# A streaming-encoder layer: the order of four engines in its first part set by tables

## The chip, the cores and the metric

The kernel runs on one core of a Trainium2 chip. The number that counts is the device time of one execution in microseconds; three executions of the kernel before took 1384.44, 1378.92 and 1384.58 us, median 1384.44. The core has these engines: TensorE (PE: matmuls and transposes; its weight loads are shown apart as PEld), VectorE (DVE), ScalarE (ACT), GpSimd (POOL) and SyncE (SP), which issues most DMAs. Each runs its own list of instructions strictly in the list's order and waits at an instruction until what it needs is there.

## The reference

One layer of an encoder, for 1024 new positions (the prompt) and 64 positions of a running stream with 512 cached ones (the sample). `z = x @ w_in` is split into columns for three groups of heads:

- fox: 6 heads of attention with a forget gate: `softmax(q k / 8 + c_t - c_s)` over the causal keys, then times v
- sgu: `gelu(u) * (tril(w_s) @ layer_norm(gelu(v)) + b_s)` in blocks of 128 positions
- sb ("stick-breaking"): 6 heads with `sigmoid(z_ts) * prod_{s<j<t} (1 - sigmoid(z_tj))`, strictly causal, then times v

The three are put side by side, normalised per head, multiplied by `w_out` and added to x with a layer norm; then come `square(relu(x @ w_up)) @ w_down` and a second layer norm. New keys, values and gates are outputs too. All of it is in float32.

## The kernel before

**Numbers in two pieces.** A float32 operand is split into a high piece (a rounded copy, fp32r) and a low one (the rest), and a product is three matmuls: high by high, high by low, low by high. So a block of weights needs a DMA into a raw buffer, a copy on ScalarE (the high piece) and a subtraction on VectorE or GpSimd (the low piece); `load_w` does it, with two raw buffers of the tag `raw` in turn:

```
nc.sync.dma_start(raw, w_in[:, 4 * g:4 * g + 4, col:col + n])
nc.scalar.activation(hi, raw, AF.Copy)
lo_sub(nc.vector if g in dve else nc.gpsimd, lo, raw, hi)
```

**The first part** (about 0 to 590 us) makes projections and attention. It is written as two generators, woven together by counted costs: F makes the projections of a pair of heads (`kv_stage`, `q_stage`), later `sgu_v` and `sgu_u`; A makes the attention of a pair for 256 queries at a time (`Unit`), and for the sample (`Sample`). Pairs are called fox0 to fox2 and sb0 to sb2 in the names. In a unit of sb, TensorE makes scores (`Ssb`, L567); VectorE adds the mask to the last 128 columns (L574); ScalarE makes sigmoids of plus and minus the scores (`sgsb` L549, `snsb` L550), the mask coming before them; VectorE runs a product scan over `snsb` (L551), GpSimd multiplies (L553); TensorE transposes (`ptsb`, L615); ScalarE copies the high piece (`pthsb`, L583), VectorE subtracts (`pthsb`, L98); TensorE multiplies with the values (`osb`: L625 and L626 use the high piece, L627 and L628 the low one); ScalarE copies out (`osbsb`, L638), TensorE transposes again (`otpsb`, L646). `softmax_rows` (L539, L542) stands in for the scan in fox. For the gating, `sgu_v` makes `g1v` and `sgvv` by steps on ScalarE, VectorE and GpSimd and splits them as `vh` and `vl`. L98 is the helper `lo_sub`, so all subtractions of low pieces have that line.

**The second part** (from 590 us) is the output projection and the two large matmuls of the MLP. Its order is not touched.

**What sets the order.** The program is traced in the woven order and handed to the tile scheduler (`TileContext(schedule_with_timeline_sim=True)`), which works out each engine's list by a simulated timeline, and puts in the semaphores. Only a few pieces are chained by hand (`in_order`), by a dependency that fixes the order on one engine and sets no semaphore.

## Time and profile before

| | |
|---|---|
| three executions | 1384.44, 1378.92, 1384.58 us |
| profiled execution | 1384.7 us, of which its span 1383.0 us |
| mean granted clock of TensorE | 0.988 |
| busy: TensorE, its weight loads | 1318.9 us (95%), 1200.2 us (87%) |
| busy: VectorE, ScalarE, GpSimd | 994.2 us (72%), 719.0 us (52%), 613.7 us (44%) |

How to read rows of the trace: a row of the timeline has start, duration, engine, line, operation, `out<-in`, and count; in brackets stands how long the engine was idle just before it, and what ended that. Buffer numbers are left out, so that `Ssb` is the scores of any sb unit. A row of the waits has engine and line, the thing waited for, total us, times and longest. A row of windows has the stretch, its length, the busy time (and count) of PE, PEld, DVE, ACT and POOL, the mean granted clock of TensorE (1.00 is full), DMA share and GB/s. Where an idle engine is not the bottleneck, its idle time costs nothing by itself.

### The profile page before, as it was taken

To read this page: it belongs to the slowest core of one execution; us is meant where nothing else is said; L and a number is where in the kernel's file an instruction comes from. 1 tells how busy PE (TensorE), PEld (TensorE's weight loads), DVE (VectorE), ACT (ScalarE), POOL (GpSimd) and SP (SyncE) were. 2 spreads that over 40 slices of the span, in tenths; PEclk is the share of its full clock that TensorE was granted. 3 is DMA by queue.
4 is the path that set the end of the run, shared out by engine and by line. 5 is a ranking of instruction groups with operands and counts; after the bars stand their busy time and mean duration, and the time that the engine had idled before them with its cause. 6 is when DMAs were issued, how large, how long until landed. Compare 5 with 4: busy or idle time off the path is not lost.

```text
span 1383.0 us, 24317 instructions
## 1 busy us (share of the span) xinstructions
PE 1318.9 (95%) x8827; PEld 1200.2 (87%) x8827; DVE 994.2 (72%) x1797; ACT 719.0 (52%) x1561; POOL 613.7 (44%) x666
## 2 busy tenths in 40 slices
PE   7999989999898998999999999999998999999996
PEld 7899989999888988778899999999976787887774
DVE  4667566576788279778885877767677777777677
ACT  4457566566556376334523322222267676766665
POOL 3221222255665446766412321221176665655557
PEclk9999999999999999999999999999999999999998
DMA  7445564231303247532244434344568344435233
GB/s 226 107 125 143 165 201 122 59 90 43 103 13 73 64 146 246 171 125 70 77 132 138 159 120 169 127 135 156 178 215 282 122 144 142 141 119 170 87 136 130
DMA packets 158048, 185.64 MB, mean 134 GB/s; under 512 B 27740, under 2 KB 116124, under 8 KB 157928
## 3 DMA queue, kind: packets, MB, share of 16 engines
q1 hardware_dynamic: 155832, 183.01, 41.7%
q8 instruction: 70, 1.15, 0.4%
q10 hardware_dynamic: 2096, 1.07, 0.3%
q14 instruction: 50, 0.41, 0.1%
HBM read 117.65 MB, written 60.10 MB: 129 GB/s over the span
## 4 chain that ended last, share of the span: by engine, by line
PE 56%; DVE 12%; DMA 11%; ACT 8%; POOL 7%; issue 5%; SPq 0%; ACTq 0%; DVEq 0%; POOLq 0%
PE zA L1310 9%; PE zD L1310 6%; PE A L1775 5%; PE kvsb L368 5%; PE mx L251 4%; PE kvfox L368 3%; PE zB L1310 3%; PE zC L1310 3%; DMA rwo<-w_out 3%; POOL wd L98 3%; DMA rd<-w_down 2%; PE D L1775 2%; POOL rd L1442 1%; DMA awa<-h_dr 1%; PE qsb L509 1%
## 5 line engine op out<-in xcount | busy, mean ns | idle before, releaser
L98 POOL TENSOR_TENSOR wa<-wr,wa 128x512 fp32r<-128x512 f32 x41 | 65.2, 1618 | 219.3 <-ACT wa L1248 219.3
L98 POOL TENSOR_TENSOR wd<-rd,wd 128x512 fp32r<-128x512 f32 x77 | 100.5, 1316 | 110.9 <-ACT wd L1248 106.3
L251 PE MATMUL mx<-xT,oTb 128*128 128x512 f32 (+1 forms) x416 | 104.1, 402 | 1.6 <-DVE oTb L98 1.6
L1310 PE MATMUL zD<-xo,ws 128*128 128x288 f32 (+1 forms) x720 | 97.5, 289 | 2.7 <-DVE h4a L1474 1.6
L1310 PE MATMUL zA<-xo,ws 128*128 128x288 f32 (+1 forms) x720 | 97.0, 289 | 0.0
L1310 PEld LDWEIGHTS zD<-xo,ws 128*128 128x128 f32 x720 | 93.5, 189 | 3.4 <-DVE h4a L1474 1.8
L1310 PEld LDWEIGHTS zA<-xo,ws 128*128 128x128 f32 x720 | 93.4, 189 | 0.0
L251 PEld LDWEIGHTS mx<-xT,oTb 128*128 128x128 f32 (+1 forms) x416 | 75.5, 187 | 20.3 <-DVE oTb L98 2.4
L1442 POOL TENSOR_TENSOR rd<-rd 128x512 f32<-128x512 f32 x56 | 79.4, 1418 | 30.2 <-DVE b L98 27.9
L368 PE MATMUL kvfox<-wkvfox,xT 128*128 128x256 f32 (+3 forms) x624 | 89.5, 291 | 2.9 <-ACT wkvfox L344 2.5
L553 POOL TENSOR_TENSOR sgsb<-sgsb,snsb 128x127 f32<-128x127 f32 (+7 forms) x48 | 58.4, 1217 | 75.6 <-DVE snsb L551 68.4
L368 PE MATMUL kvsb<-wkvsb,xT 128*128 128x256 f32 (+1 forms) x624 | 88.5, 287 | 0.0
L1248 ACT ACTIVATE wd<-rd 128x512 fp32r<-128x512 f32 x105 | 63.5, 623 | 46.7 <-POOL rd L1442 23.3
L1775 PE MATMUL A<-wd,wd 128*128 128x512 f32 x312 | 83.3, 396 | 3.2 <-DVE acc L1742 2.3
L368 PEld LDWEIGHTS kvfox<-wkvfox,xT 128*128 128x128 f32 (+1 forms) x624 | 80.8, 191 | 4.2 <-ACT wkvfox L344 2.9
L551 DVE TENSOR_TENSOR_SCAN snsb<-snsb,one 128x128 f32<-128x128 f32 (+7 forms) x48 | 72.3, 1510 | 15.3 <-ACT snsb L550 14.7
L368 PEld LDWEIGHTS kvsb<-wkvsb,xT 128*128 128x128 f32 (+1 forms) x624 | 79.4, 187 | 0.2
L1321 ACT ACTIVATE sn<-zA 128x256 f32<-128x256 f32 (+1 forms) x80 | 30.9, 389 | 89.5 <-PE zA L1310 83.0
L1775 PEld LDWEIGHTS A<-wd,wd 128*128 128x128 f32 x312 | 58.1, 188 | 19.3 <-DVE acc L1742 3.6
L1775 PE MATMUL A<-wd,h4a 128*128 128x512 f32 x240 | 64.7, 395 | 2.2 <-DVE awa L1742 1.3
L1531 ACT ACTIVATE ws<-wr 128x1024 fp32r<-128x1024 f32 x28 | 29.1, 1056 | 56.7 <-DVE wr L1260 56.7
L1775 PEld LDWEIGHTS A<-wd,h4a 128*128 128x128 f32 x240 | 44.6, 188 | 14.3 <-DVE awa L1742 1.7
(551 smaller groups left out, 3744.1 us busy)
## 6 DMA issues: line engine op xcount, KB each, us to landing
h_dr<-hh SPq DMA_DIRECT2D x30, 512.0 KB, 3.2
rd<-w_down SPq DMA_DIRECT2D x30, 512.0 KB, 4.6
wr<-w_up SPq DMA_DIRECT2D x13, 1024.0 KB, 5.5
hr<-h_dr SPq DMA_DIRECT2D x31, 384.0 KB, 4.6
h_dr<-hh SPq DMA_DIRECT2D x30, 384.0 KB, 3.6
raw<-w_in SPq DMA_DIRECT2D x44, 256.0 KB, 3.4
wo_dr<-swo SPq DMA_DIRECT2D x32, 256.0 KB, 2.4
xT<-wo_dr SPq DMA_DIRECT2D x8, 1024.0 KB, 8.0
```

What stands on the lines that cost most here:

```text
L98: eng.tensor_tensor(out, src, hi.bitcast(F32), op=ALU.subtract)
L251: nc.tensor.matmul(acc[0:m], oT[:, k, hx, 0:m], wo[k // 4][hw][:, k % 4, cs], start=(i == 0), stop=(i == len(seq) - 1))
L368: nc.tensor.matmul(acc[0:n, c0:c0 + n1 - n0], xT[k // 4][:, k % 4, c:c + n], wt[:, k, hw, n0:n1], start=(i == 0), stop=(i == len(seq) - 1))
L509: nc.tensor.matmul(acc[:, 0:w], wq[:, k, hw, :], xT[k // 4][:, k % 4, c:c + w], start=(i == 0), stop=(i == len(seq) - 1))
L551: nc.vector.tensor_tensor_scan(g[:, 0:n][:, ::-1], g[:, 0:n][:, ::-1], one.broadcast_to([P, n]), 1.0, op0=ALU.mult, op1=ALU.bypass)
L553: nc.gpsimd.tensor_tensor(s[:, 0:n - 1], s[:, 0:n - 1], g[:, 1:n], op=ALU.mult)
L1248: nc.scalar.activation(hi, raw, AF.Copy)
L1310: nc.tensor.matmul(z, w[:, hw, k], xop(s, bo, hx)[:, k, :], start=(new and k == 0 and j == 0), stop=(k == 3 and j == 2), skip_group_check= ...
L1321: nc.scalar.activation(c, z, AF.Copy)
L1442: eng.tensor_tensor(r[:, o], r[:, x], r[:, y], op=ALU.subtract)
L1531: nc.scalar.activation(ws[:, 0, q, c], src[:, q], AF.Copy)
L1775: nc.tensor.matmul(z, h[:, hx, q, o], wset[self.c % 2][q][:, hw, wb], start=((n in (0, 3) or n == 1 and self.c == 0) and q == 0 and j == 0 ...
```

## The change

After the first part has been traced, a loop goes through the instructions of TensorE, ScalarE, VectorE and GpSimd in it. It sorts them into lanes by the name of the tile that each writes, and takes them from the lanes in the order of a table, `ORDER`: `23e 24e'` means 23 instructions of lane e, then 24 of lane e' (the odd ones). Each is chained to the one before it by the same kind of dependency as in `in_order`. The arithmetic, the tiles and the buffers stay. SyncE's list and the second part are left to the scheduler. Two lines of the tables are shown, of some 80.

```
+ORDER = {}
+TICK = {"PE": {"kv": 0, "pt": 2, "sgm": 2, "mx": 1}, "ACT": {}, "DVE": {"T": 0, "sgvv": 0, "y": 0}, "POOL": {}}
+KIND = {
+    "PE": "a:S b:Ss0 c:Ss1 d:ftp e:kv f:mx g:o h:op i:os j:otp k:pk l:pkc m:pt n:ptn o:pts p:q q:sgm "
+           "r:sgu s:sgv t:wstp u:xtp",
...
+ORDER["PE"] = """
+8u e 8u 23e 24e' 8u k 8u k 14e 4u 2e' 10e 22e' 4u 8e k 4e 7u k 5u 12e 4u 14e' 2u 10e' 8e k 15e k e 14u 24e'
...
+ORDER["ACT"] = """
+2q 2y D 2y D 2y 2D h 2z h 4D g D g 2h 2D g 2D g h D h g h 2D g 2D h 2b h y g 3y b g b n b 2n f b n f 2h g 2a
...
+        traced = nc.cur_bb.bb.instructions
+        phase_1 = len(traced)
...
+        def lane_of(i, eng, code):
+            nm = i.outs[0].bass_ap.tensor.name
+            m = re.match(r"([a-zA-Z]+\\d?)_?(?:fox|sb)\\d(.*)", nm) or re.match(r"([a-zA-Z]+)(.*)", nm)
+            nums, at = re.findall(r"\\d+", m[2]), TICK[eng].get(m[1])
+            return code[m[1]] + ("'" if at is not None and at < len(nums) and int(nums[at]) % 2 else "")
+
+        for eng, e in (("PE", nc.tensor), ("ACT", nc.scalar), ("DVE", nc.vector), ("POOL", nc.gpsimd)):
+            code = dict(w.split(":")[::-1] for w in KIND[eng].split())
+            lanes = {}
+            for i in traced[phase_1:]:
+                if i.engine == e.engine:
+                    lanes.setdefault(lane_of(i, eng, code), []).append(i)
+            prev = None
+            for word in ORDER[eng].split():
+                n, k = re.match(r"(\\d*)(.*)", word).groups()
+                for _ in range(int(n or 1)):
+                    i = lanes[k].pop(0)
+                    if prev is not None:
+                        tc.add_manual_dep(i, prev.name, mybir.DependencyInfo(
+                            mybir.DependencyClass.NoSync, mybir.DependencyReason.DATA), reason="order")
+                    prev = i
+            assert not any(lanes.values()), eng
```

What the tables alter is seen when the engines' lists of both programs are laid side by side. TensorE's list is the same to the last instruction. ScalarE's differs in ten places and VectorE's in ten. GpSimd's differs mostly in that casts and subtractions of the cached values alternate, where four casts came first; SyncE's, which the scheduler still makes, has some DMAs a few places earlier or later. The ScalarE places, in order of time: at the start two small gate-weight copies go behind three large ones and two copies of x; near 113 us a weight copy goes behind an exponential; near 191 us `swo` (a copy of the output weights) goes behind `kc_fox` on ScalarE, and its VectorE step behind a `kc_fox` there; near 277, 356, 441, 446 and 484 us weight copies go two to four places later; near 439 us a `vh` comes ahead of a `g1v`; near 379 us `osbsb` comes ahead of `qssb`, near 496 us `snsb` ahead of a `qdsb`, near 530 us a `g1u` ahead of two others. On VectorE the mask of a score block comes ahead of scans or subtractions near 297, 428, 484, 494 and 523 us; near 383 to 411 us some steps of `sgvv`, `g1v` and a scan swap places; near 568 us two steps of the head norm do. In the lists below a statement's line number is 84 higher in the changed file than before.

ScalarE near 356 us, where the second half of the SGU weights `wv` is copied; `pthsb0` is the high piece of transposed attention rows, `kvssb1` and `kpsb1` are keys and values of the next pair. Before:

```order
L344 ACTIVATE wv_5078<-raw1542_1_5091 128x4x128
L583 ACTIVATE pthsb0_3_1_2_4993<-ptsb0_3_1_2_4988 128x512
L469 ACTIVATE kvssb1_8_5071<-kvsb1_8_5047 64x256
L454 ACTIVATE kpsb1_3_4668<-pksb1_6_5056 64x256
L583 ACTIVATE pthsb0_3_1_3_5004<-ptsb0_3_1_3_5000 128x384
```

And in the changed program:

```order
L667 ACTIVATE pthsb0_3_1_2_4993<-ptsb0_3_1_2_4988 128x512
L553 ACTIVATE kvssb1_8_5071<-kvsb1_8_5047 64x256
L538 ACTIVATE kpsb1_3_4668<-pksb1_6_5056 64x256
L667 ACTIVATE pthsb0_3_1_3_5004<-ptsb0_3_1_3_5000 128x384
L428 ACTIVATE wv_5078<-raw1542_1_5091 128x4x128
```

The copy of `wv` stood ahead of four others and stands behind them.

VectorE near 428 us; `Ssb1_7_1_512` is the mask's addition to the last scores of pair sb1, `snsb1_7_1` the scan of the same rows. Before:

```order
L842 TENSOR_SCALAR sgvv6_6016<-sgvv6_6016,sgst6_6022 128x256
L647 TENSOR_REDUCE otsb1_2_0_5843<-otpsb1_2_1_5984 128x2x64
L375 TENSOR_TENSOR gsv8_6147<-gsv8_6147,sgv8_6118 64x256
L843 TENSOR_TENSOR sgvv6_6016<-sgvv6_6016,gvb_5423 128x256
L98 TENSOR_TENSOR pthsb1_3_0_0_5981<-ptsb1_3_0_0_5976,pthsb1_3_0_0_5981 128x512
L98 TENSOR_TENSOR pthsb1_3_0_1_6037<-ptsb1_3_0_1_6032,pthsb1_3_0_1_6037 128x512
L574 TENSOR_TENSOR Ssb1_7_1_512_6066<-Ssb1_7_1_512_6066,m_sb_107 128x128
L551 SCALAR_TENSOR_TENSOR snsb1_7_1_6073<-snsb1_7_1_6073,one_70 128x1024
```

And in the changed program:

```order
L926 TENSOR_SCALAR sgvv6_6016<-sgvv6_6016,sgst6_6022 128x256
L658 TENSOR_TENSOR Ssb1_7_1_512_6066<-Ssb1_7_1_512_6066,m_sb_107 128x128
L731 TENSOR_REDUCE otsb1_2_0_5843<-otpsb1_2_1_5984 128x2x64
L459 TENSOR_TENSOR gsv8_6147<-gsv8_6147,sgv8_6118 64x256
L927 TENSOR_TENSOR sgvv6_6016<-sgvv6_6016,gvb_5423 128x256
L182 TENSOR_TENSOR pthsb1_3_0_0_5981<-ptsb1_3_0_0_5976,pthsb1_3_0_0_5981 128x512
L182 TENSOR_TENSOR pthsb1_3_0_1_6037<-ptsb1_3_0_1_6032,pthsb1_3_0_1_6037 128x512
L635 SCALAR_TENSOR_TENSOR snsb1_7_1_6073<-snsb1_7_1_6073,one_70 128x1024
```

The mask is five places earlier, and the five stand behind it; the scan keeps its place.

ScalarE right behind that, near 441 to 448 us; `wkvsb2` are the key and value weights of the last pair, whose raw pieces are `raw2694_0` and `raw2694_1`; `vh8_6116`, the high piece of the sample's SGU value, came next after the last row shown. Before:

```order
L344 ACTIVATE wkvsb2_6172<-raw2694_0_6181 128x4x128
L517 ACTIVATE qdsb2_1_6333<-qsb2_1_6270 64x256
L583 ACTIVATE pthsb1_3_1_0_6250<-ptsb1_3_1_0_6245 128x512
L638 ACTIVATE osbsb1_3_0_6170<-osb1_3_0_5975 128x256
L583 ACTIVATE pthsb1_3_1_1_6263<-ptsb1_3_1_1_6258 128x512
L818 ACTIVATE so7_0_6303<-sgm7_0_6299,bs_5421 128x256
L517 ACTIVATE qdsb2_1_6333<-qsb2_1_6270 64x256
L583 ACTIVATE pthsb1_3_1_2_6292<-ptsb1_3_1_2_6287 128x512
L818 ACTIVATE so7_1_6309<-sgm7_0_6299,bs_5421 128x256
L344 ACTIVATE wkvsb2_6172<-raw2694_1_6185 128x4x128
L583 ACTIVATE pthsb1_3_1_3_6344<-ptsb1_3_1_3_6340 128x384
L818 ACTIVATE so7_2_6316<-sgm7_2_6312,bs_5421 128x256
```

And in the changed program, up to `vh8_6116` and what follows it:

```order
L667 ACTIVATE pthsb1_3_1_0_6250<-ptsb1_3_1_0_6245 128x512
L722 ACTIVATE osbsb1_3_0_6170<-osb1_3_0_5975 128x256
L428 ACTIVATE wkvsb2_6172<-raw2694_0_6181 128x4x128
L667 ACTIVATE pthsb1_3_1_1_6263<-ptsb1_3_1_1_6258 128x512
L902 ACTIVATE so7_0_6303<-sgm7_0_6299,bs_5421 128x256
L601 ACTIVATE qdsb2_1_6333<-qsb2_1_6270 64x256
L667 ACTIVATE pthsb1_3_1_2_6292<-ptsb1_3_1_2_6287 128x512
L902 ACTIVATE so7_1_6309<-sgm7_0_6299,bs_5421 128x256
L667 ACTIVATE pthsb1_3_1_3_6344<-ptsb1_3_1_3_6340 128x384
L902 ACTIVATE so7_2_6316<-sgm7_2_6312,bs_5421 128x256
L931 ACTIVATE vh8_6116<-sgvv8_6146 64x256
L428 ACTIVATE wkvsb2_6172<-raw2694_1_6185 128x4x128
```

The copy of the first piece stands three places later, behind `osbsb1_3_0`; that of the second goes behind `pthsb1_3_1_3`, `so7_2` and `vh8`.

More of the change, by code (lines that the diff above doesn't have):

```diff
@@ new lines @@
+t B A g A A' t z a z 2A' r 2t i B t i a g B i A g z a i z A' z B z A a r h A 2t B w A' t A' F g t w A z w z
+t r t A w A t F t B u v 2k a B 4k 2a l k 2B a k a w B r B w a t 2s a B j a B t j w B w r a 2t x B r a t B t
+r a B t a t r B t E a B E t g a t r E B g t i E a i g E B E g i t a t i E B r t g t E B E C g C t E C r E t
+C t q C g q 2C p C p q t g q g u v J n 5C r 2C p J q C p 2s n 2q n q J' J 2p n J J' 2n 2J'
+"""
+ORDER["POOL"] = """
+e 4o 2n p n a n a 12n o m o m 4n p 2a 2n 4d 7n 4k n 4k 2n 4o 2m 2p n 4d 8n 4k 2n 4k 5n 4o 2m 2p 2n 4d 7n 4k
```

69 lines of the change are left out of this document (added).

## The prediction

> **What bounds the kernel now.** I read the page first, then the waits of TensorE, then the busy time on both sides of 590 us, where the tables end.
>
> ```profile
> span 1383.0 us, 24317 instructions
> PE 1318.9 (95%) x8827; PEld 1200.2 (87%) x8827; DVE 994.2 (72%) x1797; ACT 719.0 (52%) x1561; POOL 613.7 (44%) x666
> ...
> 0.00:590.00 590.00, 549.77 (x4246) 522.99 (x4247) 402.79 (x859) 335.04 (x831) 249.70 (x364) 0.98 0.43 124
> 590.00:1383.00 793.00, 769.15 (x4583) 677.21 (x4581) 591.37 (x939) 383.92 (x730) 364.04 (x303) 0.99 0.42 142
> ```
>
> TensorE is busy for 95% of the span, and its order and matmuls do not change. Before 590 us it stands idle for 590.00 - 549.77 = 40.2 us; that is all that an order can win there, besides stretches where TensorE runs at a lower clock. These are its waits before 590 us:
>
> ```profile
> PE osb L627 <- DVE pthsb L98: 5.4, 9, 1.7
> PE Sfox L567 <- DVE mfox L539: 5.2, 5, 2.9
> ...
> PE xtp L324 <- DMA xr<-x_prompt: 4.4, 1, 4.4
> PE kvfox L368 <- ACT wkvfox L344: 2.5, 1, 2.5
> PE sgv L368 <- DVE sgvv L767: 1.9, 1, 1.9
> ```
>
> No row is large. The waits for mfox, sgvv and the first input (11.5 us) have no moved instruction next to them. So the change is a dozen places of 0.1 to 2 us, and each has to be followed to the next wait.
>
> **Weight copies on ScalarE.** An in-order ScalarE stands before a copy whose DMA is still under way, and what TensorE wants stands behind it. The clearest case is the SGU weights:
>
> ```profile
> 356.21 0.63 ACT L344 ACTIVATE wv<-raw 128x512 fp32r<-128x512 f32 x1 [1.72 <-DMA raw<-w_in]
> 357.38 0.39 PE L625 MATMUL osb<-pthsb,vpsb 128*128 128x256 f32 x1 [0.99 <-ACT pthsb L583]
> ```
>
> ScalarE idles 1.72 us, and TensorE 0.99 us for the pthsb behind. With the copy four places later pthsb starts at its inputs: **-1.0 us** (bounds -1.0 and 0; the sgv matmuls, which use wv, waited for sgvv alone in the list above, so the copy has room). Three smaller cases are alike:
>
> ```profile
> 113.49 0.63 ACT L344 ACTIVATE wkvfox<-raw 128x512 fp32r<-128x512 f32 x1 [0.72 <-DMA raw<-w_in]
> 115.31 0.87 PE L615 MATMUL ptfox<-ident,Tfox 128*128 128x128 f32 x6 [0.17 <-ACT Tfox L542]
> 117.25 0.39 PE L625 MATMUL ofox<-pthfox,vpfox 128*128 128x256 f32 x1 [0.60 <-ACT pthfox L583]
> 190.95 0.72 ACT L997 ACTIVATE swo<-rwo,gmx 128x512 fp32r<-128x512 f32 x1 [1.37 <-DMA rwo<-w_out]
> 192.48 0.39 PE L625 MATMUL ofox<-pthfox,vpfox 128*128 128x256 f32 x1 [0.31 <-ACT pthfox L583]
> 193.69 0.39 PE L627 MATMUL ofox<-pthfox,vpfox 128*128 128x256 f32 x1 [0.22 <-DVE pthfox L98]
> ```
>
> Behind 113.49 the two waits hold 0.77 us. Tfox (L542) goes ahead of the copy and gains about half of its 0.72 + 0.63 us: **-0.4**, half of the 0.77. Behind 190.95 only kc_fox is taken out, pthfox still stands behind swo, so of 0.31 + 0.22 = 0.53 us I take **-0.4**. The fourth, at 277 us, I estimate at **-0.1** from the smallest of these waits. Bounds of the three together: -1.4 and 0.
>
> At the start two gate columns go behind the copies of the large weights. The first matmul waited 2.5 us for the last copy (the row above), and now for a gate copy: **+0.1**, up to +0.7 if a large copy finds its DMA late.
>
> **Masks and scans on VectorE.** The largest place, at 428 to 447 us:
>
> ```profile
> 427.96 0.42 DVE L647 TENSOR_REDUCE otsb<-otpsb 128x128 f32<-128x256 f32 x1
> 431.20 0.29 DVE L574 TENSOR_TENSOR Ssb<-Ssb,m_sb 128x128 f32<-128x128 f32 x1
> 432.71 2.29 DVE L551 TENSOR_TENSOR_SCAN snsb<-snsb,one 128x1024 f32<-128x1024 f32 x1 [1.22 <-ACT snsb L550]
> 439.81 0.47 PE L627 MATMUL osb<-pthsb,vpsb 128*128 128x128 f32 x1 [1.67 <-DVE pthsb L98]
> 441.29 0.63 ACT L344 ACTIVATE wkvsb<-raw 128x512 fp32r<-128x512 f32 x1 [1.25 <-DMA raw<-w_in]
> 443.13 0.69 PE L646 MATMUL otpsb<-ident,osbsb 128*128 128x128 f32 x2 [1.04 <-ACT osbsb L638]
> 446.18 0.72 POOL L844 TENSOR_TENSOR sgvv<-sgvv,gvb 64x256 f32<-64x256 f32 x1 [2.09 <-DVE sgvv L843]
> 446.85 0.62 ACT L344 ACTIVATE wkvsb<-raw 128x512 fp32r<-128x512 f32 x1
> 447.43 1.70 PE L368 MATMUL kvsb<-wkvsb,xT 128*128 128x256 f32 x13
> 448.09 0.41 ACT L847 ACTIVATE vh<-sgvv 64x256 fp32r<-64x256 f32 x1
> ```
>
> The mask goes from 431.20 to 427.96, five places up. Its sigmoids are then done before VectorE comes to the scan, and most of the scan's idle 1.22 us goes: VectorE runs about 1.1 us earlier up to the pthsb on which TensorE waits 1.67 us at 439.81. Behind that, the weight copy at 441.29 (1.25 us idle) goes behind osbsb, and most of the 1.04 us at 443.13 goes too. Together -2.1. What is late next: the second weight half (446.85) now stands behind vh of tile 8 (448.09), and vh behind the GpSimd step that ends at 446.18 + 0.72 = 446.90. The kv matmuls start at 447.43; twelve of the thirteen use the first half, the last, at 447.43 + 1.70 less one matmul or about 448.8, the second. If vh's chain comes 1.1 us earlier too, vh runs at about 445.9 and the copy ends at 445.9 + 0.41 + 0.62 = 446.9, so TensorE can gain up to 448.8 - 446.9 = 1.9 us before it waits there. The DMA of that half is issued when the first half's copy and subtraction have freed the slot; that copy's place moves down while the chain moves up, so it stays about where it was. On SyncE its issue then stands behind one more output (o_dr), whose ScalarE step is earlier as well. I take **-1.6**, bounds -2.5 (all the waits and some of the low clock below) and 0 (vh unmoved: the copy then ends at 448.09 + 0.41 + 0.62 = 449.1, 0.3 after the place where it is wanted).
>
> The other masks and scans:
>
> ```profile
> 299.72 1.64 DVE L551 TENSOR_TENSOR_SCAN snsb<-snsb,one 128x512 f32<-128x512 f32 x1 [0.83 <-ACT snsb L550]
> 302.41 0.39 PE L625 MATMUL osb<-pthsb,vpsb 128*128 128x256 f32 x1 [1.56 <-ACT osbsb L638]
> 480.88 3.01 DVE L551 TENSOR_TENSOR_SCAN snsb<-snsb,one 128x256 f32<-128x256 f32 x2
> 483.70 0.63 ACT L344 ACTIVATE wu<-raw 128x512 fp32r<-128x512 f32 x1 [2.31 <-DMA raw<-w_in]
> 488.63 1.70 PE L368 MATMUL sgu<-wu,xT 128*128 128x256 f32 x12 [1.15 <-DVE qdsb L518]
> 494.19 0.33 PE L627 MATMUL osb<-pthsb,vpsb 128*128 128x128 f32 x1 [0.38 <-DVE pthsb L98]
> 494.44 0.60 ACT L549 ACTIVATE sgsb<-Ssb 128x512 f32<-128x512 f32 x1 [1.43 <-DVE Ssb L574]
> 497.09 1.04 PE L567 MATMUL Ssb<-kpsb,qdsb 128*128 128x256 f32 x4 [1.07 <-ACT snsb L550]
> ```
>
> At 299.72 the mask now goes ahead of the scan before; VectorE's 0.83 us idle shrinks, but the mask must wait for its scores: **-0.3** of the 1.56 us (bounds -0.8, +0.3). At 483.70 the copy lets ScalarE go on, but VectorE is full from the two scans at 480.88 onward, and the 1.15 us wait hangs on VectorE: **-0.2** (bounds -1.15, 0). At 494.44 the mask goes ahead of a scan and pthsb: ScalarE's 1.43 us wait and the 1.07 us at 497.09 behind it go, the 0.38 us at 494.19 grows: **-0.6** (bounds -1.1, +0.3). At 523 us the same swap, estimated by half of that: **-0.3**.
>
> ```profile
> 379.11 0.42 PE L646 MATMUL otpsb<-ident,osbsb 128*128 128x128 f32 x2 [1.71 <-ACT osbsb L638]
> 379.74 0.19 PEld L627 LDWEIGHTS osb<-pthsb,vpsb 128*128 128x128 f32 x1 [0.18 <-DVE pthsb L98]
> ```
>
> Here osbsb goes ahead of qssb, and the 1.71 us wait gets shorter, but L627, four matmuls on, waits for VectorE until 379.74 whatever ScalarE does: **0**. The moved products in the SGU values (383 to 411 us) and the last regions (530, 568 us) stand where VectorE is full; together I estimate **-0.3**, bounds +-1.
>
> GpSimd's and SyncE's places also shift (casts and subtractions of cached values now alternate); none of the waits above ends on them, so 0, and 0.5 us if one cover goes.
>
> **Sum**: -1.0 - 0.4 - 0.4 - 0.1 + 0.1 - 1.6 - 0.3 - 0.2 - 0.6 - 0.3 + 0 - 0.3 = -5.1 us. The profiled execution took 1384.7 us (span 1383.0 and 1.7 around it), 0.3 above the median of 1384.44. Forecast: 1384.7 - 5.1 = **1379.6 us**. The bounds of the terms, all the good or all the bad ones, are -10 and +3; they will not fall together, so its own range is 1376.5 to 1382.
>
> **The clock, and the rivals.** The granted clock of TensorE halves in places:
>
> ```profile
> 185.10:188.50 3.40, 0.57 (x4) 0.57 (x5) 2.67 (x8) 2.64 (x7) 0.00 (x0) 1.00 0.48 167
> 439.30:446.10 6.80, 5.26 (x23) 4.96 (x24) 5.07 (x12) 4.23 (x10) 2.73 (x4) 0.50 0.53 122
> 497.20:500.70 3.50, 3.50 (x17) 3.50 (x18) 3.34 (x7) 2.70 (x9) 0.83 (x2) 0.52 0.17 37
> ```
>
> *More gain by the clock.* The stretches at 0.50 and 0.52 follow the very waits that shrink here (437 and 497 us). At full clock their TensorE work would take half: 5.26/2 = 2.6 and 3.50/2 = 1.75 us, 4.4 together, so 1379.6 - 4.4 = 1375.2 us. Against it: the weight copy at 447 holds the first back, and 185.10 shows 3.40 us with only 0.57 busy and the clock at 1.00, so idle alone does not decide. [...]
>
> *Stalls only move.* As at 379.74: VectorE, not the moved instruction, is behind most waits. If only 1.0 at 356 and half a microsecond elsewhere is kept, 1384.7 - 1.5 = 1383.2 us. For it: 488.63; against: the idle 1.22 us of VectorE itself.
>
> *Slower by the second weight half at 446.85.* Standing behind vh, it comes late if GpSimd or a scan of 2.29 us gets between. Once the copy starts after 448.8 - 0.6 = 448.2 us it holds the kv matmuls one for one. Three scans of 2.29 us ahead of vh's VectorE steps would make it 6.9 + 0.3 = 7.2 us late; the other places give -5.1 + 1.6 = -3.5, so 1384.7 + 3.7 = 1388.4 us. For it: GpSimd had been idle for 2.09 us at 446.18, so the chain already lags. Against it: the order puts no scan among those steps.
>
> *The tables change nothing beyond the listed moves,* or less than that: then 1384 us; the built order shows the moves, so little speaks for it.
>
> **How the numbers follow.** Forecast 0.45, more by the clock 0.22, stalls move 0.23, slower 0.07, no effect 0.03. About 0.5% (6.9 us) can be told from no change, so faster means below 1377.5: nearly all of the clock's case and a fifth of the forecast's, 0.30. Slower means above 1391.4: a third of the slower case, and 0.03 because the three times before already span 5.7 us: 0.05. Same: 0.65. The range, 1373.5 to 1385, holds the forecast, the clock's case but its end, and the case of moved stalls.
>
> **What would show it.** Right: TensorE's waits near 357 and 443 us gone, the scan of 432.71 with no idle before it, the matmul of 379.74 at the same distance to its neighbours, 488.63 little changed, idle before 590 us down from 40 to about 35 us. The clock's case: 1.00 where 439.30 and 497.20 had half. Wrong: the kv matmuls near 447 us waiting for wkvsb, or a new wait at the start above 3 us.

## The result, and the profile after

The changed kernel took 1374.78 us (median of 11 runs, 1369.80 to 1381.56); the kernel before, run beside it, 1382.22 us (11 runs, 1378.44 to 1384.95). The ratio is 0.9950 with a 95% interval of 0.9931 to 0.9969: 6.9 us faster, between 4.3 and 9.5. The ratio is not the quotient of the two medians, which would be 0.9946 (7.4 us). One execution of the kernel before, among those beside the last experiment, took 6199.27 us and is left out of all figures. The forecast was 1379.6 us, 5.1 us less than the profiled execution of before; the profiled execution of the changed kernel took 1378.24 us, 6.5 less than before's. The interval reaches to both sides of the 0.5% that can be told from no change.

The page of the changed kernel, and its busy time on both sides of 590 us:

```profile
span 1376.2 us, 24318 instructions
PE 1317.1 (96%) x8827; PEld 1200.1 (87%) x8827; DVE 996.0 (72%) x1797; ACT 719.7 (52%) x1561; POOL 617.1 (45%) x666
...
0.00:590.00 590.00, 553.52 (x4271) 527.65 (x4272) 407.83 (x865) 337.14 (x833) 258.63 (x368) 0.98 0.43 124
590.00:1376.00 786.00, 763.53 (x4558) 672.45 (x4556) 588.18 (x932) 382.52 (x729) 358.46 (x298) 1.00 0.42 143
```

TensorE's idle time in the first 590 us is 590.00 - 553.52 = 36.5 us, where it was 40.2. The mean clock there is 0.98 in both kernels; behind 590 us it is 1.00 instead of 0.99. Its waits before 590 us, the longest ones:

```profile
PE osb L711 <- DVE pthsb L182: 6.6, 7, 1.7
...
PE Sfox L651 <- DVE mfox L623: 3.8, 3, 2.5
PE kvfox L452 <- ACT wkvfox L428: 3.0, 1, 3.0
PE otpsb L730 <- ACT osbsb L722: 1.8, 2, 1.0
PE otpsb L730 <- DVE otsb L731: 1.7, 1, 1.7
```

In each row stand the sum, the number and the longest of the waits. The wait for `pthsb` of VectorE, the largest before (5.4 us in 9 waits), has grown to 6.6 in 7. What shrank is spread over many small rows.

TensorE's list is the same in both programs, so each matmul can be looked up in both traces and the difference of its start read as a running account. These starts are from the timelines of TensorE; a negative shift means that the changed kernel is ahead.

| matmul | before, us | after, us | shift |
|---|---|---|---|
| first `kvfox` | 8.89 | 9.33 | +0.44 |
| `otpfox` | 105.86 | 107.78 | +1.92 |
| scores behind the `mfox` wait | 187.93 | 189.25 | +1.32 |
| near 235 us | 235.00 | 235.07 | +0.07 |
| `osb` behind the scan at 300 us | 302.41 | 302.00 | -0.41 |
| `osb` behind the `wv` copy | 357.38 | 355.73 | -1.65 |
| `otpsb`, ScalarE's swap | 379.11 | 377.26 | -1.85 |
| near 413 us | 413.31 | 412.10 | -1.21 |
| `osb` with the 1.67 us wait | 439.81 | 438.23 | -1.58 |
| `otpsb` behind the weight copy | 443.13 | 440.04 | -3.09 |
| last `kvsb` matmul, second weight half | 448.85 | 445.84 | -3.01 |
| first `sgu` | 488.63 | 485.45 | -3.18 |
| `osb`, high piece | 494.19 | 491.06 | -3.13 |
| twelve `sgu` | 497.93 | 493.07 | -4.86 |
| `osb` behind them | 500.75 | 494.73 | -6.02 |
| `osb` | 534.86 | 528.12 | -6.74 |
| `mx`, the tables' end | 590.81 | 585.42 | -5.39 |
| end of span | 1383.0 | 1376.2 | -6.8 |

The rows of the changed kernel's timeline that answer to those of the prediction:

```profile
107.78 0.44 PE L730 MATMUL otpfox<-ident,osbfox 128*128 128x128 f32 x2 [1.62 <-ACT osbfox L722]
302.00 0.38 PE L709 MATMUL osb<-pthsb,vpsb 128*128 128x256 f32 x1 [0.77 <-ACT osbsb L722]
355.73 0.36 PE L709 MATMUL osb<-pthsb,vpsb 128*128 128x256 f32 x1
377.26 0.41 PE L730 MATMUL otpsb<-ident,osbsb 128*128 128x128 f32 x2 [1.72 <-DVE otsb L731]
406.93 0.39 PE L709 MATMUL osb<-pthsb,vpsb 128*128 128x256 f32 x1 [1.05 <-ACT pthsb L667]
438.23 0.33 PE L711 MATMUL osb<-pthsb,vpsb 128*128 128x128 f32 x1 [1.67 <-DVE pthsb L182]
440.04 0.63 PE L730 MATMUL otpsb<-ident,osbsb 128*128 128x128 f32 x2
445.84 0.39 PE L452 MATMUL kvsb<-wkvsb,xT 128*128 128x256 f32 x1 [0.37 <-ACT wkvsb L428]
485.45 1.70 PE L452 MATMUL sgu<-wu,xT 128*128 128x256 f32 x12 [0.65 <-DVE qdsb L602]
491.06 0.33 PE L711 MATMUL osb<-pthsb,vpsb 128*128 128x128 f32 x1 [0.54 <-DVE pthsb L182]
493.07 1.69 PE L452 MATMUL sgu<-wu,xT 128*128 128x256 f32 x12
```

Gone are the waits at 357 us (0.99), 443 us (1.04) and 497 us (1.07), smaller the ones at 302 (1.56 to 0.77) and 488 us (1.15 to 0.65). The 1.67 us at 439 is the same to the hundredth, the 1.71 at 379 now has another releaser, and at 445.84 and 406.93 there are new ones. The first 235 us gave nothing: the account starts with a loss of 1.9 us and is back at zero there. Behind the tables' end the account gains another 1.4 us (-5.4 at `mx`, -6.8 at the end of the span), 1.2 of it idle time of TensorE in a part whose order was not touched; in the kernels below that part alone differs from before's by +1.0 to -3.7 us. So a difference of a few us between two executions is no proof of an order; what the moves themselves do is compared step by step over all kernels in the section on the prediction.

### The profile page after: what moved, and what is told of

It reads as the page before. It is cut to its first block, busy times and chain, and to the rows that moved or that the text cites. A ratio compares the mean times of both kernels' runs of the same rounds, so it can differ in the third digit from the quotient of the medians.

```text
span 1376.2 us, 24318 instructions
## 1 busy us (share of the span) xinstructions
PE 1317.1 (96%) x8827; PEld 1200.1 (87%) x8827; DVE 996.0 (72%) x1797; ACT 719.7 (52%) x1561; POOL 617.1 (45%) x666
## 3 DMA queue, kind: packets, MB, share of 16 engines
q8 instruction: 70, 1.15, 0.4%
q10 hardware_dynamic: 2096, 1.07, 0.3%
## 4 chain that ended last, share of the span: by engine, by line
PE 56%; DVE 14%; DMA 10%; ACT 8%; POOL 7%; issue 5%; SPq 0%; ACTq 0%; DVEq 0%; POOLq 0%
PE zA L1419 9%; PE zD L1419 6%; PE mx L335 5%; PE kvsb L452 5%; PE A L1884 5%; PE kvfox L452 3%; PE zB L1419 3%; DMA rwo<-w_out 3%; PE zC L1419 3%; DMA rd<-w_down 2%; PE D L1884 2%; POOL wd L182 2%; PE qsb L593 2%; DVE snsb L635 1%; POOL rd L1551 1%
```

## The experiments

The theories were these. *The listed places*: the gain is the sum of the stalls that the moved masks and weight copies take away, each where the prediction put it. *The clock*: the stalls matter less than the half-speed stretches behind them. *Stalls move*: VectorE and GpSimd set the pace, and what is taken away in one place stands in the next. All kernels compute the whole result. A kernel with before's order written as tables carries single moves; line numbers differ by one to three from kernel to kernel. Ratios are to the kernel before, run on the same chip, with 95% intervals; 0.001 is 1.4 us. Like the ratio above they are not quotients of medians. Where two experiments are compared through their ratios, the intervals are added in quadrature.

### Masks alone

Before's order, with the five masks on VectorE (297, 428, 484, 494, 523 us) and ScalarE's swap of `snsb` and `qdsb` at 496 us. The place at 494 us:

```diff
 DVE scan snsb_3_0
 DVE knsb
+DVE mask Ssb_3_1_0
 DVE scan snsb_2_1
 DVE subtraction pthsb_0_1_0
-DVE mask Ssb_3_1_0
```

> Only the five masks on VectorE (297, 428, 484, 494, 523 us) and the ScalarE swap near 496 us are in their new places; all other lists are as before. By the sum of the prediction: -0.3 - 1.1 (the mask's part of 428 us) - 0.2 - 0.6 - 0.3 = -2.5 us, 1382.2 - 2.5 = 1379.7, and TensorE's step at 439.81 comes 1.1 us earlier against its neighbours ahead of 428 us. By the new reading of the changed trace (GpSimd's power step and the scan get in each other's way there): only -0.4 at 439.81, but -1.5 at 497.09, together about -2.6. If stalls only move: under -0.5. If the clock is behind the gain: -2 to -4, with the stretch at 497 us at full clock.

Measured: 1378.00 us, ratio 0.9983 (0.9970 to 0.9996), 2.3 us faster. Timeline of this kernel:

```profile
298.58 0.39 PE L710 MATMUL osb<-pthsb,vpsb 128*128 128x256 f32 x1 [0.75 <-ACT osbsb L723]
437.36 0.33 PE L712 MATMUL osb<-pthsb,vpsb 128*128 128x128 f32 x1 [1.67 <-DVE pthsb L183]
438.91 0.63 ACT L429 ACTIVATE wkvsb<-raw 128x512 fp32r<-128x512 f32 x1 [1.31 <-DMA raw<-w_in]
440.74 0.69 PE L731 MATMUL otpsb<-ident,osbsb 128*128 128x128 f32 x2 [1.71 <-ACT osbsb L723]
```

The mask at 297 us works: the wait behind it is 0.75 us instead of 1.56. At 428 us the mask alone gains nothing that lasts: 437.36 still waits 1.67 us, and at 440.74 the wait behind the weight copy has become longer, 1.71 us instead of 1.04, because the copy still stands ahead of `osbsb` and its DMA comes no earlier.

### Weight copies alone

Before's order, with the moved weight copies (113, 191, 277, 356, 441, 446 and 484 us). At 441 us:

```diff
-ACT wkvsb, first half
 ACT qdsb
 ACT pthsb_3_1_0
 ACT osbsb_3_0
+ACT wkvsb, first half
```

> Only the weight copies on ScalarE are later (113, 191 with its VectorE step, 277, 356, 441, 446, 484 us); masks and all else as before. By the sum: -0.4 - 0.4 - 0.1 - 1.0 - 0.2, and -0.5 to -1.2 at 443 us, -2.6 to -3.3 us, so about 1379.3; the matmul of 357.38 without a wait, and the first user of the second half of wkvsb2 (448.85) waiting little. If stalls only move: -1 at most, a new wait of the same size within 5 us behind each place. If the second half behind vh is the next bound (the slower rival): a wait over 1 us at 448.85.

Measured: 1378.28 us, ratio 0.9973 (0.9958 to 0.9988), 3.7 us faster. Timeline of this kernel:

```profile
353.57 0.36 PE L710 MATMUL osb<-pthsb,vpsb 128*128 128x256 f32 x1
437.91 0.63 PE L731 MATMUL otpsb<-ident,osbsb 128*128 128x128 f32 x2
443.47 0.39 PE L453 MATMUL kvsb<-wkvsb,xT 128*128 128x256 f32 x1 [0.40 <-ACT wkvsb L429]
```

At 356 us TensorE gains 1.23 us on the matmul before, at 441 us 1.24 us, and both waits are gone, with no mask moved. The second weight half makes TensorE wait 0.40 us at 443.47: here too it is the next bound.

### All other moves alone

Before's order with what is in neither of the two: the gate copies at the start, the swaps at 379, 439 and 530 us, the products of the SGU values at 383 to 411 us, the head norm at 568 us and GpSimd's casts.

> Only the moves to which the prediction gave about nothing: the gate copies at the start, osbsb ahead of qssb (379 us), vh ahead of g1v (439 us), g1u (530 us), the VectorE steps of the SGU values (383 to 411 us) and of the head norm (568 us), and GpSimd's alternating casts. By the sum: +0.1 + 0 - 0.3, so 1382 +- 1. By the changed trace: +0.4 to +1.3 at the start, +0.4 at 383 to 411 us, so 1383 to 1384.

Measured: 1383.51 us, ratio 1.0019 (1.0005 to 1.0033), 2.6 us slower. The timeline shows a first matmul that starts at 9.30 us behind a wait of 2.99 for ScalarE, and two waits near 410 us:

```profile
408.22 0.50 PE L897 MATMUL sgm<-vh,wst 128*128 128x256 f32 x2 [0.41 <-DVE sgvv L850]
411.89 0.44 PE L767 MATMUL pkcsb<-ident,cache_sb_k 128*128 128x128 f32 x2 [1.37 <-DVE otsb L730]
```

The profiled execution of this kernel, 1380.75 us, is the fastest of its twelve, so its trace can hardly show where the loss lies. The three parts add to -2.3 - 3.7 + 2.6 = -3.4 us, against -6.9 of the whole. Their intervals reach 1.8 to 2.1 us to each side, so the sum is known to about 3.4 us and the difference of 3.5 us to about 4.3: whether the parts add up is not decided.

### The change without the place at 428 to 448 us

The changed kernel with before's order there: VectorE's mask, ScalarE's `vh` and `g1v`, both halves of `wkvsb`.

> The changed kernel with the moves of 428 to 448 us alone taken back (the mask, vh4 and g1v8, both halves of wkvsb2). By the sum it loses 1.6 us: 1374.8 + 1.6 = 1376.4, and TensorE loses 1.6 to 1.8 us between 428 and 450 us and keeps the rest. If stalls only move, it loses under 0.5.

Measured: 1377.76 us, ratio 0.9969 (0.9957 to 0.9982). Timeline of this kernel:

```profile
438.99 0.47 PE L710 MATMUL osb<-pthsb,vpsb 128*128 128x128 f32 x1 [1.67 <-DVE pthsb L181]
442.35 0.69 PE L729 MATMUL otpsb<-ident,osbsb 128*128 128x128 f32 x2 [1.08 <-ACT osbsb L721]
```

The wait behind the weight copy is back (1.08 us), the 1.67 us is there as always. By the ratios the place is worth 0.0019, 2.6 us, known to 3.2; by the account of TensorE's starts 3.01 - 1.21 = 1.8 us between 413 and 449 us.

### The change without the start, without the SGU products, without all other moves

The question was what makes the other moves 2.6 us slower. First the changed kernel with before's order at the start alone (ScalarE's copies of the gate columns and of x, the subtractions on GpSimd):

```diff
+ACT wkvfox gate columns, head
 ACT wkvfox raw_0
+ACT xT, first
+ACT wkvfox gate columns, tail
 ACT wkvfox raw_1
```

> The changed kernel with the start alone taken back: the two gate copies on ScalarE and their subtractions on GpSimd stand where they stood before. If the start is what made the leftover moves slower, it gains 0.4 us at the first matmul and up to 1 us more because full clock then comes earlier: 1374.8 - 1 = 1373.8. If the start costs only the +0.1 of the prediction, no difference.

Measured: 1375.18 us, ratio 0.9945 (0.9924 to 0.9966).

Then with before's order of the SGU products on VectorE, 383 to 411 us:

> The changed kernel with the VectorE moves of 383 to 411 us alone taken back (the low half of wst, the products of sgvv, g1v and a scan). If they are what made the leftover moves slower, it gains 1 to 2 us on the changed kernel, 1373 to 1374, and TensorE has no wait of 1.05 us at 406.93. If they cost nothing, as the prediction has it, no difference.

Measured: 1375.35 us, ratio 0.9948 (0.9929 to 0.9967).

Then without all of them:

> The changed kernel with all the moves that the prediction gave about nothing taken back (start, 379, 383 to 411, 530, 568 us, GpSimd's alternating casts), except vh4 ahead of g1v8, which belongs to 428 to 448 us. If the parts add up as they were measured alone (masks -2.4, weight copies -3.7, the leftover moves +2.6 us), it gains 2.6 us on the changed kernel: about 1372. If the parts only work together, it is no faster than the changed kernel, 1374.8, or slower.

Measured: 1375.28 us, ratio 0.9936 (0.9916 to 0.9957). All three are the changed kernel's 0.9950 within their intervals. So the other moves bring nothing in the whole change, and no one of the two larger groups costs what they cost together in before's order. The account of starts gives 0.5 us to the start and 0.4 to the SGU products in the kernel with all other moves alone, 0.9 us together, inside the 0.7 to 4.6 measured; where the rest of the 2.6 us is stays open.

### The output weights behind the attention weights

In the changed kernel and in the one without the other moves the next waits before 200 us stand behind copies of the output weights `swo` on ScalarE:

```profile
190.49 0.74 PE L652 MATMUL Sfox<-kpfox,qdfox 128*128 128x256 f32 x4 [2.70 <-DVE mfox L624]
108.94 0.44 PE L731 MATMUL otpfox<-ident,osbfox 128*128 128x128 f32 x2 [1.69 <-ACT osbfox L723]
```

These rows are from the timeline of the kernel without the other moves; in the changed kernel the waits are 2.5 (the `mfox` row of its waits) and 1.62 us. The wait near 107 us is not the order's alone: the kernels without the place at 428 us and without the start, whose order is the same there, do not lose these 1.3 us. The obvious step is the change's own: move the copy (and VectorE's step for it) behind what TensorE wants.

```diff
-ACT swo_1 (107 us)
 ACT osbfox_2_0
 ACT kvsfox_7
 ACT pthfox_2_1_0
 ACT pthfox_2_1_1
+ACT swo_1
...
-ACT swo_1 (186 us)
 ACT kc_fox_0
 ACT osbfox_2_1
...
 ACT pthfox_3_0_1
+ACT swo_1
```

> The changed kernel, and two copies of output weights (swo1_1 near 107 us, swo5_1 near 186 us in its profile) stand behind the attention work that is ready, on ScalarE and on VectorE. TensorE's waits of 1.62 us (otpfox) and 2.47 us (Sfox behind mfox) should go, 3 to 4 us: 1371 to 1372. If stalls only move, the later output weights hold the next copy, and the gain is under 1 us.

Measured: 1382.01 us, ratio 0.9995 (0.9979 to 1.0011): all of the gain is lost, 6.2 us (known to 3.4) against the changed kernel. Both waits are gone, and this stands in their place in the timeline (the row SPq is the issue of a load on SyncE's queue):

```profile
188.31 0.42 SPq L1073 DMA_DIRECT2D rwo<-w_out  x1
192.24 0.72 ACT L1080 ACTIVATE swo<-rwo,gmx 128x512 fp32r<-128x512 f32 x1 [4.08 <-DMA rwo<-w_out]
193.50 0.58 PE L708 MATMUL ofox<-pthfox,vpfox 128*128 128x256 f32 x1 [3.87 <-ACT pthfox L666]
```

The load of the next raw piece is issued at 188.31, when the one before is done with (VectorE's step for it ends at 187.65), and arrives 3.9 us later. The next `swo` copy keeps its place in ScalarE's list, so ScalarE idles 4.08 us before it, and TensorE 3.87 us for the `pthfox` behind it. Counted from 184 us against the kernel before, TensorE is 3.1 us ahead at the scores behind the `mfox` wait and 3.3 us late at 210 us: besides the 3.87 us, slower matmuls behind it (`ofox` takes 0.42 us at 193.88, where 187.28 shows 0.28; in the changed kernel it takes 0.41 at a clock of 0.50) cost about 1 us and a wait near 208 us another 1.1. A copy moved back pushes the DMA that it frees, and that DMA's own copy is now the one that comes too early in the list.

A gentler form starts from the kernel without the other moves: the same copies a few places back, the next copy behind one `pthfox` on ScalarE, but VectorE's step for it left in place.

> As norest (the masks, the weight copies, vh4), and the output weights in a gentler way than in swo: only work that is ready before their DMA lands goes ahead of swo1_1 and swo5_1, so that their buffer comes free as early as before, and swo6_0 goes behind the pthfox that TensorE waited for. TensorE's waits near 107 us (up to 1.6) and 187 us (2.5) should go without the wait of 3.9 us that swo made at 193 us: 3 us below norest, 1371 to 1372. If the wait only moves to the next weights again: no gain on norest (1374 to 1375).

Measured: 1377.36 us, ratio 0.9959 (0.9945 to 0.9973). The wait has changed its engine, as the timeline of this kernel shows:

```profile
191.62 0.72 ACT L1082 ACTIVATE swo<-rwo,gmx 128x512 fp32r<-128x512 f32 x1 [3.17 <-DMA rwo<-w_out]
192.38 0.75 DVE L1083 SCALAR_TENSOR_TENSOR swo<-rwo,gmx,swo 128x512 fp32r<-128x512 f32 x1 [3.51 <-ACT swo L1082]
193.79 0.58 PE L712 MATMUL ofox<-pthfox,vpfox 128*128 128x256 f32 x1 [3.73 <-DVE pthfox L183]
```

VectorE's step for `swo` waits 3.51 us for ScalarE's, and TensorE 3.73 us for the `pthfox` on VectorE behind it. Against the kernel under it (ratio 0.9936) this is 3.2 us more, known to 3.4: nothing was gained.

### The raw weights of the last pair in a free buffer

On top of that kernel, the raw pieces of the last pair's weights go into another buffer, so that their load is not held by the slot, and one more `pthsb` goes ahead of `g1v`:

```diff
-load_w(w, P, ..., "vp" if st is pairs[1] else "raw", dve=dve)
+load_w(w, P, ..., "vp" if st in (pairs[1], pairs[4]) else "raw", dve=dve)
```

> best2, and for the last pair's second half of weights (raw2694) two buffers of another tag, so that its DMAs need not wait for the raw buffers, and the third pthsb1_3_0 goes ahead of g1v8 on VectorE. If the second half is the bound behind 440 us, as the 0.37 us wait at 445.84 of the changed kernel says, that wait goes and TensorE gains 1 to 1.5 us between 428 and 450 us on best2. If VectorE is the bound there, nothing is gained.

Measured: 1379.83 us, ratio 0.9977 (0.9959 to 0.9994), 2.5 us more than the kernel under it, known to 3.1. The wait at the 1.67 us place fell to 0.80 us, but 0.69 us followed right behind, and the wait for the second weight half did not go (0.53 us, 0.24 in the kernel under it). The copy of that half does not wait for its load there: it starts at 448.76 us right behind `vh`, for which ScalarE had waited 0.73 us on GpSimd's `sgvv`. That chain through VectorE and GpSimd, not the load, is what comes last. Between 428 and 449 us TensorE gains 1.7 us on before, as in the kernel under it: nothing was gained.

### GpSimd's small steps ahead of the scan

At 428 us VectorE's scan and a GpSimd step overlap in the changed kernel, and both take longer: 2.76 us instead of 2.29, and 2.55 instead of 0.56 (shown below). Here two small GpSimd steps on `sgst7` go ahead of its `wkvsb` subtraction:

```diff
+POOL sgst7 add
+POOL sgst7 power
 POOL wkvsb subtraction
-POOL sgst7 add
 POOL sgvv6 add
-POOL sgst7 power
```

> The changed kernel, and GpSimd's two steps for the variance of tile 7 (an addition and a power) stand ahead of the subtraction of wkvsb2's first piece, so ahead of the scan near 430 us. If the collision with GpSimd's power step ate the mask's gain there, the scan takes 2.3 us instead of 2.76, the power step 0.6 instead of 2.55, and TensorE's step that came at 438.23 comes 0.5 to 0.8 us earlier against the steps ahead of 428 us; the time gains as much at most, which the runs can hardly tell. If another GpSimd step takes its place beside the scan, the scan stays at 2.7 us and nothing is gained.

Measured: 1378.13 us, ratio 0.9967 (0.9952 to 0.9983); nothing was gained (0.0017 above the changed kernel, known to 0.0025). The timeline of this kernel stands in the last section.

### The next copy behind `pthfox` on both engines

The kernel without the other moves, with the `swo` copies back, and the next `swo` behind `pthfox_3_1_1` on ScalarE and VectorE alike:

```diff
-DVE swo_0 (192 us)
 DVE pthfox_3_0_2
 DVE pthfox_3_0_3
...
 DVE pthfox_3_1_1
+DVE swo_0
```

> norest, and swo1_1 and swo5_1 behind attention work that is ready, as in swo and best2; but swo6_0, whose DMA starts only when swo5_1 has been stored and on which ScalarE and VectorE waited 3 to 4 us in swo and best2, goes behind the pthfox copies of the next unit on both engines. If the waits at 107 and 187 us can be had without a new one, TensorE is 4 us ahead of norest at 210 us and the time is 1370 to 1371. If the wait finds a third place again (the next output weights, or a store in SyncE's list), the time stays at 1374 to 1377 and the lesson is that these copies are one chain of DMAs, not a matter of places.

Measured: 1372.53 us (6 runs, 1371.91 to 1377.52), ratio 0.9929 (0.9910 to 0.9949). Timeline of this kernel:

```profile
104.67 0.38 PE L731 MATMUL otpfox<-ident,osbfox 128*128 128x128 f32 x2
...
186.59 0.44 PE L769 MATMUL pkcfox<-ident,cache_fox_k 128*128 128x128 f32 x2 [2.13 <-DVE kc_fox L183]
```

The wait of 1.69 us near 107 is gone and the 3.7 us near 193 too; 2.13 us for `kc_fox`, behind `swo` on VectorE, are new. It has the lowest median of all kernels here, but its interval overlaps that of the change: faster than before by 7 to 12 us is shown, faster than the change is not, nor faster than the kernel under it (1.0 us by the ratios, known to 3.9). In this execution the moves do not pay: between 184 and 210 us it loses 1.8 us against before, where the kernel under it loses 0.1, with `ofox` matmuls that take 0.41 or 0.42 us from 188.37 to 191.85 us, as they do at a clock of 0.50, and 0.28 at 187.54.

## Why the prediction was right, and where its steps were not

The forecast of -5.1 us lies inside the measured -4.3 to -9.5. Since TensorE's list is the same in all kernels, the change of the account over a place can be read in every trace, against the one of before: a step that the kernels with a move show, and the others do not, belongs to the move. There are thirteen kernels beside the one before.

| place, from and to in before's time | forecast | kernels with the move | kernels without it |
|---|---|---|---|
| start (gate copies), 4.45 to 8.89 | +0.1 | +0.5 (six) | 0.0 to +0.1 (seven) |
| 277 (weight copy), 277.58 to 278.04 | -0.1 | -0.32 (eleven), lost again by 281 us | +0.1 (two) |
| 300 (mask), 300.04 to 302.41 | -0.3 | -0.8 (eleven) | 0.0 (two) |
| 356 (`wv` copy), 350.06 to 360.05 | -1.0 | -1.3 (eleven) | +0.1 and +0.3 (masks alone) |
| SGU products, 390.03 to 414.54 | in -0.3 | +0.4 to +0.5 (four), -0.1 (two) | 0.0 (seven) |
| 428 (mask and weight copies), 428.00 to 448.85 | -1.6 | -1.2 to -1.9 (nine); copies alone -1.4, masks alone +0.5 | 0.0 (two) |
| 488 (mask and `wu` copy), 480.07 to 488.63 | -0.2 | -0.3 (ten, mask and copy both moved) | 0.0 (none or the mask moved), -0.06 (copies alone) |
| 497 (mask and `snsb`), 494.19 to 497.09 | -0.6 | -1.5 (eleven) | 0.0 (two) |
| 523 (mask), 523.04 to 530.23 | -0.3 | -0.6 (eleven) | 0.0 (two) |

The six places from 300 to 523 us that hold make -0.8 - 1.3 - 1.7 - 0.3 - 1.5 - 0.6 = -6.2 us in the changed kernel, where the forecast had -4.0; the start and the SGU products cost it 0.5 us each, so these rows give about -5.2. That each step comes with its move and is absent without it shows the cause. That the sum comes so near to -5.1 is luck in part: the terms that hold were too small, 0.9 us of others did not hold, and the start and the SGU products cost 1 us where about nothing was forecast. The steps in its order:

**What bounds it.** Right: the win is idle time of TensorE before 590 us, which fell from 40.2 to 36.5 us, where about 35 were named. That is 3.7 us of the 5.4 by which `mx` came earlier; the other 1.7 us are matmuls that took less time themselves, 1.07 of it the twelve `sgu` at 497 us, a difference to which the order has no claim (see the rivals).

**The `wv` copy at 356 us, -1.0.** Right: -1.24 in the changed kernel, -1.23 with the copies alone, the wait gone.

**113, 191 and 277 us, -0.9 together.** Not shown. Kernels in which these copies were not moved get ahead at the same places: near 115 us by 0.5 (masks alone) and 0.4 us (other moves alone; the changed kernel 0.35), near 193 us by 0.5 (masks alone; the changed kernel 0.2, the copies alone 1.1). So the waits of 0.17 to 0.60 us on which the terms were built belong to one execution of before more than to its order; a late DMA is the likely reason, which no run tested. At 277 us the move does what was forecast, but the 0.32 us are lost again by 281 us.

**The start, +0.1.** The first matmul waits 2.98 us instead of 2.5 (+0.44 by its start), inside the +0.7 allowed. All six kernels with these moves have it; by the times the kernel without the start's moves is no faster, which 0.5 us would not show.

**428 to 448 us, -1.6.** The size came out (-1.8 in the account, 2.6 known to 3.2 in the runs); the step inside it that failed is "VectorE runs about 1.1 us earlier up to the pthsb on which TensorE waits 1.67 us". The timeline of before there, GpSimd and the transposes behind it:

```profile
431.95 0.56 POOL L841 TENSOR_TENSOR sgst<-sgst,negh 128x1 f32<-128x1 f32 x1
433.24 2.29 POOL L98 TENSOR_TENSOR vl<-sgvv,vh 128x256 fp32r<-128x256 f32 x1 [0.73 <-ACT vh L847]
435.50 2.04 POOL L553 TENSOR_TENSOR sgsb<-sgsb,snsb 128x1023 f32<-128x1023 f32 x1
437.59 0.55 PE L615 MATMUL ptsb<-ident,sgsb 128*128 128x128 f32 x3 [0.21 <-POOL sgsb L553]
```

And the timeline of the changed kernel, GpSimd and the scan on VectorE:

```profile
430.00 0.73 POOL L928 TENSOR_TENSOR sgvv<-sgvv,gvb 128x256 f32<-128x256 f32 x1
430.11 2.76 DVE L635 TENSOR_TENSOR_SCAN snsb<-snsb,one 128x1024 f32<-128x1024 f32 x1
430.69 2.55 POOL L925 TENSOR_TENSOR sgst<-sgst,negh 128x1 f32<-128x1 f32 x1
433.21 0.73 POOL L182 TENSOR_TENSOR vl<-sgvv,vh 128x256 fp32r<-128x256 f32 x1
433.90 2.05 POOL L637 TENSOR_TENSOR sgsb<-sgsb,snsb 128x1023 f32<-128x1023 f32 x1
```

The mask did its part: the scan begins at 430.11 where it began at 432.71, and ends at 432.87 instead of 435.00, 2.1 us earlier, 0.9 of it beyond the lead of 1.21 us that TensorE already had at 413 us. But what TensorE transposes next is GpSimd's product `sgsb` of that scan, and it stands behind `vl` in GpSimd's list. Before it began 0.50 us behind the scan's end (435.50), now 1.03 us (433.90): 1.6 us earlier, 0.4 beyond the lead. The matmuls ahead of the 1.67 us wait hang on that product, and the one that waits does so on a `pthsb` made from it; all move together, so the wait keeps its length (1.67 us in the changed kernel and in those with masks alone, without this place and with GpSimd's steps moved) and the matmul gains 1.58 - 1.21 = 0.4 us. The other 1.5 us of the place are the weight copy's at 443 us; the copies alone show 1.24 of it. The next bound was named rightly: the last `kvsb` matmul waits 0.37 us for the second weight half, which ScalarE copies behind `vh` (timeline of the changed kernel):

```profile
444.85 0.42 ACT L931 ACTIVATE vh<-sgvv 64x256 fp32r<-64x256 f32 x1 [0.25 <-POOL sgvv L928]
445.17 0.61 ACT L428 ACTIVATE wkvsb<-raw 128x512 fp32r<-128x512 f32 x1
```

**299.72, -0.3; 488, -0.2; 494 and 497, -0.6; 523, -0.3.** Right in mechanism and too small: -0.8, -0.3, -1.5 and -0.6 by the table. At 488 us neither the mask nor the copy alone brings it, only both. At 497 us both waits were taken to trade against each other; 0.38 grew only to 0.54 while 1.07 went altogether.

**379 us, 0.** Right, with another releaser than named: `otsb` of VectorE instead of `pthsb`, 1.72 us for 1.71; the account moves by 0.2 us there, and by as much in the kernels with masks or copies alone. As the prediction had it, ScalarE was not what came last.

**The rest, -0.3.** Wrong in sign when taken alone (+2.6 us, 0.7 to 4.6), nothing in the whole; cause open. In the trace the account first gains 1.5 us between 398 and 402 us, where before had a half-speed stretch, and then loses 2.2 between 406 and 414 us, of it 1.46 in two waits (1.05 at 406.93 and one of 0.41 behind it), the rest in a half-speed stretch of its own that begins at 407.85. What stays is the +0.5 us of the table, and the kernel with before's order of the SGU products is not faster by its time.

**The rivals.** *More by the clock* fell as an explanation of the time. At 497 us it looks as described: the twelve `sgu` matmuls take 1.69 us at full clock where they took 2.76 at half. But all thirteen kernels gain 1.4 to 1.5 us between 497.09 and 500.75, the copies alone and the other moves alone too, in which TensorE waits 1.08 us there as before: the stretch was one of that execution of before, not of its order. And the changed kernel has half-speed stretches too, at 189.40 us and again at 438.60, as its windows show (the third number from the end is the clock):

```profile
189.40:192.80 3.40, 3.40 (x17) 3.40 (x18) 3.27 (x9) 1.91 (x5) 0.00 (x0) 0.50 0.66 169
438.60:442.00 3.40, 3.40 (x18) 3.40 (x18) 2.96 (x8) 2.60 (x6) 1.53 (x3) 0.50 0.53 130
491.90:495.30 3.40, 3.40 (x30) 3.26 (x28) 3.31 (x8) 3.35 (x11) 1.09 (x1) 1.00 0.35 77
```

Both executions have five ahead of the last 15 us of the span, 23.9 us in all before and 20.5 after. Over all timed runs the mean granted clock is 0.9890 before (91 runs) and 0.9901 after (11): 0.0011 of 1376 us is 1.5 us if every microsecond were TensorE's, and among the runs of before 0.001 of clock goes with only 0.43 us, which makes 0.5 of the 6.9 us. *Stalls only move* fell for the change (more than 1.5 us was kept) but is what decided the moved `swo` copies. *Slower by the second half* stayed at 0.37 us. *No effect* lies outside the interval.

**The bounds.** The profiled execution of before, 1384.7 us, is slower than the median of the runs beside the changed kernel, 1382.2, and some of its waits were chance: a step of about -1 us near 227 us, where no kernel moves anything, stands in nine of the thirteen and not in the other four, and one of -0.5 near 235 us in five. Between 535 and 591 us the changed kernel loses 1.4 us of its lead again, and the six others with the moves at 530 and 568 us lose 0.3 to 1.5 us; the six kernels without them lie between -0.7 and +0.9. The ranges overlap, so a cost of these moves is not told from chance. A sum of twelve waits of one execution carries that.

## What to carry to other kernels

Before a step is moved ahead of a wait, follow its result through every engine to the matmul that waits: a scan 2.1 us earlier was worth 0.4 us, because the product on a third engine stood behind another instruction there. A weight copy that makes an in-order engine stand for its DMA (ScalarE for 1.72 us at 356 us) is the surer place, as long as the DMA that the copy itself releases still has time (here 3.9 us) before its own copy comes in the list. Waits of a few tenths of a microsecond next to DMAs should be seen in a second execution before a term is built on them. And where one list is the same in several kernels, its starts, compared place by place between those with a move and those without it, tell the move's own part from chance of one execution.

## What the hardware showed beyond that

**A scan and a GpSimd instruction that overlap.** Before, the 128x1024 scan took 2.29 us, and GpSimd's `vl`, begun within it at 433.24, took 2.29 us too and ended at 435.53, 0.5 us behind the scan's end; the same `vl` took 0.73 us after. In the changed kernel the scan issued at 430.11 while GpSimd's addition ran until 430.73, and took 2.76 us; GpSimd's 128x1 step begun at 430.69 took 2.55 us instead of 0.56, until 433.24. With that step moved out of the way, the next one takes its place (timeline of the kernel with GpSimd's small steps moved):

```profile
427.48 0.57 POOL L924 TENSOR_TENSOR sgst<-sgst,negh 128x1 f32<-128x1 f32 x1
...
428.74 2.70 DVE L634 TENSOR_TENSOR_SCAN snsb<-snsb,one 128x1024 f32<-128x1024 f32 x1
429.25 2.72 POOL L927 TENSOR_TENSOR sgvv<-sgvv,gvb 128x256 f32<-128x256 f32 x1
```

The small step is at 0.57 us again, and `sgvv`'s addition takes 2.72 us instead of 0.73. So the cost in these rows is one instruction of GpSimd that begins within the scan, whichever of these three it was (it ends 0.37 to 0.53 us behind the scan), and 0.41 and 0.47 us of the scan in the two kernels in which GpSimd was still at another step as the scan issued. With none at work as it issued, the scan of before took 2.29 us beside `vl`. What holds the two up, the rows do not show.

**Half-speed stretches do not follow the single wait.** The stretches at a clock of 0.50 last 3.41 or 6.83 us, five in each of the two profiled executions (one more begins as the work runs out, at 1374.54 and 1370.41 us). Three of the five begin near the same places in both (70.65, 439.29 and 548.51 us before, 69.93, 438.57 and 544.38 after), two do not (398.33 and 497.31 before, 189.40 and 407.85 after). The full clock itself began at 12.62 us before and at 15.32 after (17 matmuls ran in the 3.62 us ahead of it and 29 in the 3.38 us behind it before, 17 in 3.42 and 30 in 3.38 after). After, the stretch at 189.40 follows a wait of 2.47 us and the one at 438.57 a wait of 1.67; before, the one at 439.29 begins within a wait of 1.67 and the one at 497.31 follows a wait of 1.07. But the longer wait of before, 2.92 us up to 187.93, was not followed by one: the clock stayed at 1.00. So the length of the wait does not account for them.

The two traces show more. In both, every change of the granted clock lies a whole number of 3.413 us behind the first one, so the span can be cut into pieces of that length, and TensorE's busy time be counted in each:

| TensorE busy in a piece at full clock, both traces | such pieces | half clock in the next one |
|---|---|---|
| under 48% (1.64 us) | 7 | 7 |
| 48 to 64% | 18 | 5 |
| over 64% (2.18 us) | 758 | 0 |

In the changed kernel it was busy for 0.94 us in the piece from 185.99 to 189.40, and for 1.52 us in the one that ends at 438.57. Before, the piece ahead of 497.31 held 2.04 us (60%), and half clock followed. The stretch of 185.10 to 188.50 in the prediction, with only 0.57 us, lies across two pieces, which held 1.72 us (50%) and 2.15 (63%), and the clock stayed. So in these two traces the busy time of a piece goes with the clock of the next one, and the length of a single wait does not. Between 48 and 64% they do not tell what decides.
